# Expert down weights: two neighbouring matrix rows in each partition of a slot, and hidden units transposed in that order

## Chip, cores and metric

The kernel runs on one core of one Trainium2 chip. The metric is the device time of one execution, in microseconds; less is better.

## What is computed

One block of a hybrid backbone on 256 latent tokens and 256 context tokens with a model width of 1024: modulated norm, input projection, retention and latent attention, a gated merge, an output projection with a residual, and then a mixture of experts. The change lies in the experts alone. Each token goes to 4 of 32 experts, and an expert computes, for its tokens xb:

```
gu = xb @ w_gu[e] + b_gu[e]                  # w_gu[e]: 1024 x 2048, gate and up side by side
gate, up = gu[:, :1024], gu[:, 1024:]
gate = minimum(gate, 7);  up = clip(up, -7, 7)
glu = gate * sigmoid(1.702 * gate)
y = ((up + 1) * glu) @ w_down[e] + b_down[e] # w_down[e]: 1024 x 1024
```

The outputs are weighted with the softmax of the four router values, summed per token, added to the residual and normed. All weights are float32, so an expert reads 8 MB for `w_gu` and 4 MB for `w_down`; the 32 experts read 384 MB.

## The kernel before

**Stages.** The program first does modulation, projections, attention, retention, merge, residual and router (up to about 580 us in the profile). Then a loop runs over the 32 experts, one after the other. At the end the last expert's product is done by columns, so that its output can be added and normed in pieces.

**Tokens of an expert.** Each expert has 64 slots for tokens (`CAP`). Matrix products that give 64 rows are paired: one product writes the upper 64 partitions of a PSUM bank and the other the lower 64, with different columns of the weights. So after `gate_up` the tile `up` holds on partitions 0 to 63 the hidden units 0 to 511 of the 64 slots, and on partitions 64 to 127 the units 512 to 1023.

**Weights.** The weights of the experts come in tiles `w` of 128 partitions x 2048 numbers, 1 MB each, twelve per expert. `load_gu` (line 1067) fetches 128 rows of `w_gu`, one row of 8 KB per partition, eight tiles per expert. `load_down` (line 1072) fetches 256 rows of `w_down`, four tiles per expert: rows 256 j to 256 j + 127 go to the first half of the partitions' 8 KB, rows 256 j + 128 to 256 j + 255 to the second half, 4 KB each. The last tile of the last expert is fetched by `load_last` (line 1079) in two DMAs of 512 KB, one for each half. All of these are issued from SP's queue, in the fixed order of the list `todo`: eight gate and up tiles, four down tiles, expert after expert. A tile is fetched when its slot in the ring of buffers (`slots`) is free again; several experts' tiles fit in the ring, so SP runs ahead of the products.

**An expert.** `gate_up` multiplies the gathered tokens with eight tiles (line 1444, eight products a tile), with the previous expert's output added to the tokens on the way (`combine`, line 1426). VectorE and ScalarE then make `up` from the two banks (lines 1448 to 1452). `down` calls `hidden`, which transposes `up` in four blocks of 128 columns on TensorE (the `transpose` of line 147) into one PSUM bank and copies it to the tile `hT` (named `ga`); while these run, TensorE begins the next expert's banks with its biases (line 1307). A block c gives hidden units 128 c on (from the upper slots) and 512 + 128 c on (from the lower ones), one unit per partition, and `hidden` returns the eight 64-column pieces of it in the order of the units. `down` then runs through the four down tiles: half r of tile j is multiplied with piece f = 2 j + r (line 1473, sixteen pairs of products). The last expert uses line 1595 for this in place of line 1473.

**Order.** The order of TensorE's instructions is the order in which the code is written; the other engines' queues are ordered by the framework's scheduler in the expert loop. `order` rows below show both programs' queues.

Of the kernel before, what the change touches and what calls it, by code (L numbers as in the profile page):

```python
# [26 lines left out]
CAP = 64  # L27
# [32 lines left out]
def hybrid_block(ctx: ExitStack, tc: tile.TileContext, A, out, dbg=None):  # L60
# [88 lines left out]
    def rsqrt(p, ss, n, mul, name="rs_y"):  # L149
        """(ss * mul + EPS) ** -0.5"""  # L150
        v = p.tile([128, n], F32, name="rs_v")
        w = p.tile([128, n], F32, name="rs_w")
        y = p.tile([128, n], F32, name=name)
        t = p.tile([128, n], F32, name="rs_t")
        b = p.tile([128, n], I32, name="rs_b")
        nc.vector.tensor_scalar(v, ss, mul, EPS, op0=OP.mult, op1=OP.add)
        nc.vector.tensor_scalar(b, v.bitcast(I32), 1, None, op0=OP.logical_shift_right)
        nc.vector.tensor_scalar(w, v, -0.5, None, op0=OP.mult)
        nc.vector.tensor_tensor(y.bitcast(I32), magic[:, :n], b, op=OP.subtract)
        for _ in range(3):  # L160
            if n > 2:
                nc.vector.tensor_tensor(t, y, y, op=OP.mult)
                nc.vector.tensor_tensor(t, t, w, op=OP.mult)
                nc.vector.scalar_tensor_tensor(y, t, 1.5, y, op0=OP.add, op1=OP.mult)
                continue
            for i in range(n):
                c = slice(i, i + 1)
                nc.vector.scalar_tensor_tensor(t[:, c], y[:, c], w[:, c], y[:, c], op0=OP.mult, op1=OP.mult)
            for i in range(n):
                c = slice(i, i + 1)  # L170
                nc.vector.scalar_tensor_tensor(y[:, c], t[:, c], 1.5, y[:, c], op0=OP.add, op1=OP.mult)
        return y

# [18 lines left out]
    # ada[32 g + r]: (shift, scale) of columns 0.., then 512..; then gate, gate, shift, shift; scale, scale, gate, gate  # L192
# [4 lines left out]
    # The work up to the output projection is a list of steps; those with weights get them loaded and split ahead.  # L197
# [6 lines left out]
    def run_steps():  # L204
        specs = [s for s, _ in steps if s]
        loads = [[]]
        for s in specs:
            loads[-1].append(s)
            if not callable(s):
                loads.append([])  # L210
        loaded, ready = [], []
        at = [0]

        def split_next():
            w, nk, n, raw = loaded[len(ready)]
            if raw:
                ready.append((w,))
            else:
                ready.append([y[:, :nk * n].rearrange("p (k n) -> p k n", k=nk) for y in split(w[:, :nk * n], nk * n)])

        def split_to(n):
            """the next n weights after the current ones, not counting those used as they are"""
            while len(ready) <= at[0]:
                split_next()
            while len(ready) < len(loaded) and sum(len(r) == 2 for r in ready[at[0] + 1:]) < n:
                split_next()

        ahead.append(split_to)
        for spec, fn in steps:
            while len(loaded) < min(at[0] + WR, len(loads) - 1):  # L230
                *others, weight = loads[len(loaded)]
                for other in others:
                    other()
                loaded.append(load(*weight))
            if fn is None:
                continue
            if spec is None:
                fn()
                continue
            split_to(ahead[0])  # L240
            fn(*ready[at[0]])
            at[0] += 1
        steps.clear()

    def load(src, r0, nk, pieces, raw=False):
        """rows r0.. (nk blocks of 128), the columns of all pieces side by side"""
# [72 lines left out]
    def ada_step(q, k):  # L319
        """columns 2048 (q + 1).. of the modulation, rows 128 k.."""  # L320
# [59 lines left out]
    def project(pieces, jobs, kks, mid=None, at=None):  # L380
        """jobs: (bank, part of it, token tile, first column, end column of the loaded ones, starts its bank)"""
# [20 lines left out]
    def matmul2(names, wname, r0, c0, src, k0, first, last):  # L402
        """256 rows from r0 of a weight matrix, 512 columns, against the blocks k0.. of transposed tokens"""
        def f(hi, lo):
            ah, al = src()
            for t in range(2):
                s = slice(128 * t, 128 * t + 128)
                for k in range(2):
                    mm3(B[names[t]], (ah[:, k0 + k, s], al[:, k0 + k, s]), (hi[:, k], lo[:, k]),
                        start=(first and k == 0), stop=(last and k == 1))  # L410
        step(f, (A[wname][0], r0, 2, [(c0, 512)]))
# [13 lines left out]
    def keep_warm(n):  # L425
        """work without a result: TensorE's clock falls while it waits"""
# [53 lines left out]
    M = {}  # L480

    def open_mla():
        dump("mod1", mod1)
        nc.sync.dma_start(tabm, A["tables"][:, 1024:1536])
        # a quarter of the biases of expert e in row 32 q + e
# [113 lines left out]
    def q_up(quad, kks):  # L599
        """queries of four heads: the transposed parts without positions, and the rotated ones"""  # L600
# [42 lines left out]
    def q_rot(pair):  # L643
        """the rotated parts: the high parts in the upper 64 rows, what they lack in the lower"""
# [34 lines left out]
    def scores(pair):  # L679
        """softmax of both heads, for both token tiles"""  # L680
# [83 lines left out]
    def log_decay():  # L764
        """log_sigmoid(r) = min(r, 0) - log1p(exp(-|r|)), log1p(e) = 2 atanh(e / (2 + e))"""
# [41 lines left out]
    def open_ret():  # L807
# [13 lines left out]
        # the normed tokens as rows, in the two parts  # L821
# [14 lines left out]
    def r_rows():  # L836
        """the normed, gated output of a head, transposed and split"""
# [110 lines left out]
    # scores against the normed tokens first, then the value columns of w_in  # L948
# [33 lines left out]
    def gate_ret_out(c):  # L982
        """the heads so far and the other branch, gated; the gate stays for the last head"""
# [72 lines left out]
    slots = []  # L1056

    def add_ring(n, order=None, others=(), **kw):
        """n slots for the experts' weights and others, in the order in which their space gets free"""
# [10 lines left out]
    def load_down(wdn, j):  # L1070
        w = wtile()
        nc.sync.dma_start(w.rearrange("p (r n) -> p r n", r=2),
                          wdn[256 * j:256 * j + 256].rearrange("(r p) n -> p r n", p=128))
        return w

    def load_last(wdn, j):
        w = wtile()
        for r in range(2):
            nc.sync.dma_start(w[:, 1024 * r:1024 * r + 1024], wdn[256 * j + 128 * r:256 * j + 128 * r + 128])
# [11 lines left out]
    def take(f, src, i):  # L1091
        """the next weights of the experts in their order, or others"""
# [79 lines left out]
    def router_weights():  # L1172
        """logits = rstd * (x2 @ (scale * router_w)) + shift @ router_w + router_b"""
# [65 lines left out]
    def split3(parts, src, rest):  # L1239
        """three bfloat16 parts whose sum is src; what is returned does the last two"""  # L1240
# [43 lines left out]
    def one_hot(oh, pos, ne):  # L1284
        """which token is in which slot of ne experts; pos: [128, 2, ne]"""
# [16 lines left out]
    def gu_bias(pick_row):  # L1302
        """banks for the first layer of an expert, begun with its biases; pick_row(q) picks their quarter q"""
# [13 lines left out]
    # top four: all above the fourth value, then the first of those equal to it  # L1317
# [17 lines left out]
    # position of a token among those of its expert, -1 where it isn't sent there  # L1335
# [15 lines left out]
    # gates: softmax over the four  # L1351
# [20 lines left out]
    def slot_scale(oh, ne):  # L1372
        """the norm's factor of the token in each slot, on all partitions"""
# [10 lines left out]
    def gather(oh, rb, xg, k4, ne):  # L1384
        """blocks 4 k4.. of the normed, modulated, transposed tokens in those slots"""
# [23 lines left out]
    def slot_rows(oh, i):  # L1409
        """slots of an expert against tokens, on both halves of the partitions"""  # L1410
# [9 lines left out]
    def combine(ys, ct, g=None, n=CAP):  # L1420
        """add the n rows of the sum of ys to their tokens, weighted with the gates g: [128, 2]"""
# [13 lines left out]
    def gate_up(wgu, halves, xg, i, mid=None):  # L1435
        """one block of CAP tokens of an expert, slot i of xg; mid: other work on the way"""
# [18 lines left out]
    def hidden(up, mid=None):  # L1455
        ps = pt_((128, 4, 128))
        for c in range(4):
            transpose(ps[:, c], up[:, 128 * c:128 * c + 128])
# [18 lines left out]
    def weigh(pys):  # L1477
        """the parts of an expert's output, weighted with the gate of the tokens' update, in two parts"""
# [31 lines left out]
    # biases of the second layer: one more expert whose slots are the experts  # L1510
# [101 lines left out]
    # tokens beyond the first CAP of an expert, CAP at a time  # L1612
# [64 lines left out]
```

## Time and profile before

| what | value |
|---|---|
| time, median of 3 runs | 1525.47 us (1523.48 to 1526.0) |
| span of the profiled execution | 1526.6 us |
| TensorE products busy (ends modelled) | 1427.5 us, 94% |
| VectorE / ScalarE / GpSimd busy | 614.0 / 345.9 / 77.6 us |
| read from memory | 490.02 MB |
| SP's DMA queue, share of the 16 DMA engines' span | 82.1% |
| mean granted clock of TensorE | 0.991 |

The profile has no time of its own beside the span: the span from the first to the last instruction of the profiled execution is 1526.6 us, 1.1 us above the median of the runs, and the time of a run is taken to move as the span does. TensorE's 94% is not a sign that it is the limit: products are pipelined and their ends are modelled, so that a product that is drawn out by a late operand still counts as busy. The shares are means over the whole span, in which the part before the experts and the experts have different limits.

### The profile page before, as it was taken

Reading aid. Unit: us, or ns where it says so; the run is one execution under the profiler, and the core shown is the slowest. Engines: PE = TensorE matmul, PEld = TensorE weight load, DVE = VectorE, ACT = ScalarE, POOL = GpSimd, SP = SyncE. Lnnn points to the kernel's source line nnn. Section 1 sums busy time; section 2 is a strip of 40 time slices with the busy share of each in tenths; the row PEclk is TensorE's granted clock in tenths of the full one; section 3 lists DMA queues with packets and bytes.
Section 4 is the critical chain, followed back from the end, with each engine's and each line's share of the span. In section 5 each row is a group of like instructions: output and inputs, shape, how many; then the busy total and the mean of one; then the engine's idle time right before and its main releaser. Section 6 shows DMA issues by size and latency. Waiting matters only on the chain.

```text
span 1526.6 us, 19528 instructions
## 1 busy us (share of the span) xinstructions
PE 1427.5 (94%) x7977; PEld 761.8 (50%) x7977; DVE 614.0 (40%) x1079; ACT 345.9 (23%) x606; POOL 77.6 (5%) x98
## 2 busy tenths in 40 slices
PE   8999999999999998999999998899898889898985
PEld 4676787888888774333333333333332333233323
DVE  4486645556476573332322332222322232223223
ACT  4354533444344341010110101100110011001001
POOL 3100040101010020000000000000000000000000
PEclk9999999999999999999999999999999999999998
DMA  8635364354548877999999999999999999999994
GB/s 314 200 108 169 135 207 134 111 173 130 170 120 287 314 288 282 415 415 418 416 415 417 416 417 415 416 418 417 415 417 416 417 415 418 417 415 416 417 417 183
DMA packets 117658, 492.42 MB, mean 323 GB/s; under 512 B 9488, under 2 KB 19789, under 8 KB 84793
## 3 DMA queue, kind: packets, MB, share of 16 engines
q1 hardware_dynamic: 116616, 489.23, 82.1%
q0 software_dynamic: 544, 1.21, 0.3%
q8 instruction: 64, 1.05, 0.3%
q10 hardware_dynamic: 400, 0.66, 0.1%
q14 instruction: 34, 0.27, 0.0%
HBM read 490.02 MB, written 1.05 MB: 322 GB/s over the span
## 4 chain that ended last, share of the span: by engine, by line
PE 61%; DMA 29%; DVE 7%; issue 1%; ACT 1%; POOL 0%; DVEq 0%; ACTq 0%; SPq 0%
DMA w<-in_exp_w_gu_dram 26%; PE ps L1444 12%; PE ps L276 9%; PE ps L277 9%; PE ps L278 9%; PE ps L1473 9%; PE ps L1307 4%; PE ps L147 3%; DMA w<-in_exp_w_down_dram 3%; DVE up L1452 1%; DVE up L1450 1%; PE ps L299 1%; PE ps L330 1%; DVE up L1451 1%; PE ps L287 1%
## 5 line engine op out<-in xcount | busy, mean ns | idle before, releaser
L1444 PE MATMUL ps<-w,xg 128*64 128x512 f32 x2048 | 473.6, 599 | 44.8 <-DMA w<-in_exp_w_gu_dram 43.7
L1444 PEld LDWEIGHTS ps<-w,xg 128*64 128x64 f32 x2048 | 134.3, 136 | 361.2 <-issue 215.5
L1473 PE MATMUL ps<-w,ga 128*64 128x512 f32 x992 | 218.7, 593 | 0.0
L268 DVE TENSOR_TENSOR ws<-w,ws 128x1024 fp32r<-128x1024 f32 (+2 forms) x114 | 138.9, 1225 | 74.1 <-ACT ws L267 71.4
L1433 DVE SCALAR_TENSOR_TENSOR x<-ps,gate,x 128x512 f32<-128x512 f32 x124 | 84.5, 744 | 200.2 <-PE ps L1426 200.2
L1473 PEld LDWEIGHTS ps<-w,ga 128*64 128x64 f32 x992 | 71.6, 138 | 142.6 <-issue 140.8
L267 ACT ACTIVATE ws<-w 128x1024 fp32r<-128x1024 f32 (+2 forms) x114 | 116.9, 1027 | 96.9 <-PE ps L278 82.1
L1449 ACT ACTIVATE ps<-ga 128x512 f32<-128x512 f32 x32 | 19.3, 602 | 492.7 <-DVE ga L1448 492.7
L1482 DVE TENSOR_TENSOR ps<-ps,gate 128x512 f32<-128x512 f32 (+1 forms) x33 | 22.6, 684 | 267.3 <-PE ps L1473 258.4
L277 PE MATMUL ps<-ws,hh 128*128 128x512 f32 (+3 forms) x304 | 108.8, 358 | 3.7 <-DVE ws L268 3.7
L276 PE MATMUL ps<-ws,hh 128*128 128x512 f32 (+3 forms) x304 | 109.3, 360 | 0.0
L278 PE MATMUL ps<-ws,hl 128*128 128x512 f32 (+3 forms) x304 | 108.7, 357 | 0.4 <-DVE hl L375 0.4
L1448 DVE TENSOR_SCALAR ga<-ps 128x512 f32<-128x512 f32 x32 | 22.1, 692 | 169.5 <-PE ps L1444 169.5
L272 ACT ACTIVATE up<-ps 128x512 fp32r<-128x512 f32 (+1 forms) x33 | 19.3, 584 | 260.7 <-DVE ps L1482 260.6
L277 PEld LDWEIGHTS ps<-ws,hh 128*128 128x128 f32 x304 | 57.1, 188 | 13.2 <-DVE ws L268 5.0
L276 PEld LDWEIGHTS ps<-ws,hh 128*128 128x128 f32 x304 | 57.1, 188 | 12.8 <-issue 4.4
L1307 PE MATMUL ps<-bgu,ident 128*64 128x512 f32 x256 | 63.2, 615 | 0.0
L278 PEld LDWEIGHTS ps<-ws,hl 128*128 128x128 f32 x304 | 57.1, 188 | 8.2 <-DVE hl L375 0.7
L147 PE MATMUL ps<-ident,up 128*128 128x128 f32 x128 | 20.9, 286 | 22.9 <-DVE up L1452 22.9
L1393 PE MATMUL ps<-oh,acc_m 128*128 128x128 bf16 x512 | 40.5, 223 | 0.0
L278 PE MATMUL ps<-ath,htl 128*128 128x256 f32 x128 | 35.8, 280 | 0.0
L276 PE MATMUL ps<-ath,hth 128*128 128x256 f32 x128 | 35.7, 279 | 0.0
(381 smaller groups left out, 1794.4 us busy)
## 6 DMA issues: line engine op xcount, KB each, us to landing
w<-in_exp_w_gu_dram SPq DMA_DIRECT2D x256, 1024.0 KB, 19.9
w<-in_exp_w_down_dram SPq DMA_DIRECT2D x127, 1024.0 KB, 20.0
w<-in_ada_w_dram SPq DMA_DIRECT2D x48, 512.0 KB, 4.5
w<-in_w_in_dram SPq DMA_DIRECT2D x48, 512.0 KB, 4.3
w<-in_w_in_dram SPq DMA_DIRECT2D x32, 256.0 KB, 5.2
w<-in_w_branch_ret_dram SPq DMA_DIRECT2D x16, 512.0 KB, 4.6
w<-in_w_branch_mla_dram SPq DMA_DIRECT2D x8, 512.0 KB, 5.1
w<-in_w_out_dram SPq DMA_DIRECT2D x8, 512.0 KB, 11.9
```

The lines of the kernel that those rows point to most:

```text
L147: nc.tensor.transpose(dst, src, ident[:n, :n])
L267: nc.scalar.activation(hi[:, :n], src, AF.Copy)
L268: nc.vector.tensor_tensor(lo[:, :n], src, hi[:, :n].bitcast(F32), op=OP.subtract)
L276: nc.tensor.matmul(ps, a[0], b[0], start=start, stop=False, skip_group_check=True)
L277: nc.tensor.matmul(ps, a[0], b[1], start=False, stop=False, skip_group_check=True)
L278: nc.tensor.matmul(ps, a[1], b[0], start=False, stop=stop, skip_group_check=True)
L1307: nc.tensor.matmul(ps[64 * h:64 * h + 64], pick_row(c // 512).to_broadcast([128, CAP]), bgu, start=True, stop=False, skip_group_check=True)
L1393: nc.tensor.matmul(ps[:, i, :w], part[:, t, ks], rhs, start=(t + p + i == 0), stop=(t + p == 3), skip_group_check=True)
L1433: nc.vector.scalar_tensor_tensor(a, pss[h], g[:, t:t + 1], a, op0=OP.mult, op1=OP.add)
L1444: nc.tensor.matmul(ps[64 * h:64 * h + 64], xg[k // 4][:, k % 4, sl], w[:, c:c + 512], start=False, stop=(k == KD - 1), skip_group_check=True)
L1473: nc.tensor.matmul(py[64 * h:64 * h + 64], hT[f], w[:, 1024 * r + 512 * h:1024 * r + 512 * h + 512], start=(f == 0), stop=(f == KD - 1))
L1482: nc.vector.tensor_tensor(py, py, gate2[:, cs], op=OP.mult)
```

## The change

`load_down` takes 256 consecutive rows of `w_down` as pairs: partition p gets rows 256 j + 2 p and 256 j + 2 p + 1, which lie beside each other in memory, as one run of 8 KB. `load_last` does the same in its two halves: its first DMA takes the even rows of the 256, the second the odd ones, each row still 4 KB. Since half r of a tile now holds the rows 256 j + 2 p + r, the hidden units have to stand on the partitions in that order: `hidden` transposes, for block c, every second column of `up`, starting at column 256 (c // 2) + c % 2, in place of 128 consecutive columns. The pieces, the products and their number stay. The changed file has no comments and doc strings, which shifts no line before `hidden` and two lines behind it.

```diff
     def load_down(wdn, j):
         w = wtile()
-        nc.sync.dma_start(w.rearrange("p (r n) -> p r n", r=2),
-                          wdn[256 * j:256 * j + 256].rearrange("(r p) n -> p r n", p=128))
+        nc.sync.dma_start(w, wdn[256 * j:256 * j + 256].rearrange("(p r) n -> p (r n)", r=2))
         return w

     def load_last(wdn, j):
         w = wtile()
+        rows = wdn[256 * j:256 * j + 256].rearrange("(p r) n -> p r n", r=2)
         for r in range(2):
-            nc.sync.dma_start(w[:, 1024 * r:1024 * r + 1024], wdn[256 * j + 128 * r:256 * j + 128 * r + 128])
+            nc.sync.dma_start(w[:, 1024 * r:1024 * r + 1024], rows[:, r])
         return w
...
     def hidden(up, mid=None):
         ps = pt_((128, 4, 128))
+
+        pairs = up.rearrange("s (j p r) -> s j r p", j=2, r=2)
         for c in range(4):
-            transpose(ps[:, c], up[:, 128 * c:128 * c + 128])
+            transpose(ps[:, c], pairs[:, c // 2, c % 2])
         if mid:
             mid()
```

No instruction is added, removed or moved on any engine. On SP's queue, where the experts' first down tile stands between the last tiles of the output projection (`w_out`, line 258), the DMA of line 1072 has another shape:

```order
 L258 DMA w_4841<-in_w_out_dram 128x2x512
 L1067 DMA w<-in_exp_w_gu_dram 128x2048 x2
-L1072 DMA w<-in_exp_w_down_dram 128x2x1024
+L1072 DMA w<-in_exp_w_down_dram 128x2048
 L258 DMA w_4963<-in_w_out_dram 128x2x512
 L258 DMA w_4980<-in_w_out_dram 128x2x512
```

The tile is written as one run of 2048 numbers per partition, which is the shape of the gate and up tiles of line 1067; its place in the queue is the old one.

On TensorE's queue, at the place where an expert's `hidden` and `down` meet the next expert's `gate_up`, the rows are these (`ident` is the unit matrix, `bgu` the biases, `ga` the tile hT):

```order
 L147 MATMUL ps<-ident,up 128x128 x4
 L1307 MATMUL ps<-bgu,ident 64x512 x4
-L1473 MATMUL ps<-w,ga 64x512 x16
+L1475 MATMUL ps<-w,ga 64x512 x16
 L1444 MATMUL ps<-w,xg 64x512 x16
 L1426 MATMUL ps<-up,ct 128x512 x2
```

Only the line's number differs. The four transposes of line 147 stand where they did, with the same shapes; that they read every second number of `up` does not show in the rows.

## Rows read from the trace of the kernel before

**Rows 1.** The page: the span, and DMA load in 40 slices.
```profile
span 1526.6 us, 19528 instructions
...
DMA  8635364354548877999999999999999999999994
GB/s 314 200 108 169 135 207 134 111 173 130 170 120 287 314 288 282 415 415 418 416 415 417 416 417 415 416 418 417 415 417 416 417 415 418 417 415 416 417 417 183
```

**Rows 2.** The chain, 1000 to 1070 us: start, length, what.
```profile
1021.76 19.88 DMA w<-in_exp_w_gu_dram
...
1051.87 19.91 DMA w<-in_exp_w_gu_dram
```

**Rows 3.** DMA packets by size; DMA issues: count, KB each, us to landing.
```profile
DMA packets 117658, 492.42 MB, mean 323 GB/s; under 512 B 9488, under 2 KB 19789, under 8 KB 84793
...
w<-in_exp_w_gu_dram SPq DMA_DIRECT2D x256, 1024.0 KB, 19.9
w<-in_exp_w_down_dram SPq DMA_DIRECT2D x127, 1024.0 KB, 20.0
```

**Rows 4.** Waits of SP's queue: us in total, times, longest.
```profile
SPq L1072 <- DMA w<-in_exp_w_gu_dram: 218.6, 106, 3.4
SPq L1067 <- DMA w<-in_exp_w_down_dram: 215.7, 106, 3.6
```

**Rows 5.** SP's issues, one tile each: start, length of the issue, line.
```profile
589.40 0.34 SPq L1067 DMA_DIRECT2D w<-in_exp_w_gu_dram  x1
...
1004.42 4.11 SPq L1067 DMA_DIRECT2D w<-in_exp_w_gu_dram  x1
...
1011.58 0.56 SPq L1067 DMA_DIRECT2D w<-in_exp_w_gu_dram  x1
...
1021.76 0.33 SPq L1067 DMA_DIRECT2D w<-in_exp_w_gu_dram  x1
...
1024.25 0.38 SPq L1072 DMA_DIRECT2D w<-in_exp_w_down_dram  x1
...
1031.72 1.83 SPq L1072 DMA_DIRECT2D w<-in_exp_w_down_dram  x1
```

**Rows 6.** Two stretches: us, then busy us (count) by engine, clock, DMA share, GB/s.
```profile
656.75:673.75 17.00, 17.00 (x84) 5.87 (x82) 3.43 (x6) 0.71 (x2) 0.00 (x0) 1.00 1.01 416
...
779.00:794.50 15.50, 14.53 (x94) 5.99 (x92) 6.93 (x12) 2.26 (x5) 0.00 (x0) 1.00 1.02 421
```

**Rows 7.** Two other stretches, the same columns.
```profile
767.25:774.50 7.25, 7.25 (x36) 2.43 (x34) 1.39 (x2) 0.60 (x1) 0.00 (x0) 1.00 1.03 408
...
1041.50:1045.75 4.25, 3.83 (x42) 2.40 (x42) 2.63 (x4) 1.07 (x3) 0.00 (x0) 1.00 1.03 411
```

**Rows 8.** Two stretches at the start of the experts, the same columns.
```profile
580.00:590.00 10.00, 10.00 (x67) 4.77 (x66) 2.84 (x8) 1.99 (x5) 0.00 (x0) 0.94 0.45 138
590.00:600.00 10.00, 9.78 (x54) 3.59 (x50) 3.87 (x7) 1.40 (x4) 0.00 (x0) 1.00 1.03 419
```

**Rows 9.** The chain, 600 to 700 us, at the transposes.
```profile
628.04 0.66 PE ps L147 x4
...
654.76 0.66 PE ps L147 x4
```

**Rows 10.** Groups by line, 900 to 1490 us.
```profile
L1444 PE MATMUL ps<-w,xg 128*64 128x512 f32 x1250 | 297.1, 602 | 43.6 <-DMA w<-in_exp_w_gu_dram 42.6
...
L147 PE MATMUL ps<-ident,up 128*128 128x128 f32 x76 | 12.4, 286 | 14.7 <-DVE up L1452 14.7
...
L147 PEld LDWEIGHTS ps<-ident,up 128*128 128x128 f32 x76 | 7.9, 140 | 18.0 <-DVE up L1452 15.5 <-issue 2.4
```

**Rows 11.** The chain in the last expert.
```profile
1476.86 19.86 DMA w<-in_exp_w_gu_dram
...
1501.79 0.44 PE ps L147 x4
...
1503.13 6.65 PE ps L1595 x60
```

## Prediction

> **What bounds the kernel now.** I read the page's slices first [rows 1]. Up to slice 16 (610 us; a slice is 38.2 us) the DMA engines are half idle; from there to the end they are 90% busy or more and move 415 to 418 GB/s in every full slice, whatever the other engines do. A rate that stays this flat over 23 slices is a limit of its own, so I looked at the experts as a stream of DMAs. Two stretches at its start show where it becomes full: 138 GB/s from 580 to 590 us, 419 GB/s in the ten microseconds after [rows 8]. The 25th issue of an expert's tile is at 589.40 [rows 5], so the tiles of the first two experts (24) came mostly ahead of the full stream, and all from the third expert on are in it.
>
> The chain says the same in the middle of the experts: a last gate and up tile is issued at 1021.76 and lands 19.88 us later, the next expert's is issued at 1051.87 and takes 19.91 [rows 2]. One expert thus takes 1071.78 - 1041.64 = 30.14 us, or 2.51 us for each of twelve tiles of 1 MB, and the 19.9 us in which a tile is on its way are eight such steps: eight tiles are queued. What releases SP is in its waits: line 1072 waits for gate and up tiles and line 1067 for down tiles, 106 times each [rows 4], that is, an issue waits for the landing of the tile eight issues before it.
>
> Is TensorE near that limit? Early in the loop, while it still lives on tiles fetched ahead, it goes from one expert's transposes to the next's in 654.76 - 628.04 = 26.72 us [rows 9], which is its own pace. Later it waits for the tiles: 42.6 us in 590 us, some 2.2 us per expert by a view that counts drawn-out products as busy [rows 10]. So the experts are bound by the DMA stream, with TensorE some 3 us per expert below it.
>
> **Part one: the down tiles as runs of 8 KB.** The tiles of both matrices have the same bytes, but not the same packets. Of 117658 packets 32865 are of 8 KB or more; the gate and up tiles account for 256 x 128 = 32768 of them, so they travel as one packet per partition and the down tiles as two of 4 KB [rows 3]. Does that cost time? The steps of SP's queue give the landings one by one. The issue at 1011.58 was released by the last gate and up tile, the one at 1021.76 by the fourth down tile after it, the one at 1031.72 by the fourth gate and up tile of the next expert [rows 5]. Four down tiles took 10.18 us, 2.545 each; four gate and up tiles took 9.96 us, 2.490 each. That is 0.055 us for each down tile. The period gives a second value: twelve tiles at 2.490 would take 29.88 us, against 30.14 that is 0.26 per expert or 0.065 per down tile. I take 0.0575, nearer to the direct one, because the period also holds the steps in which both kinds are under way.
>
> A third view bounds it. In ten stretches in which the packet records are of 8 KB alone the rate is 416 to 421 GB/s; in nine with 4 KB alone it is 408 to 411; the lowest and the highest of each stand in [rows 6, 7]. A megabyte takes 2.521 to 2.491 us in the first and 2.570 to 2.551 in the second, so the difference lies between 0.030 and 0.079 us.
>
> After the change the DMA of line 1072 has the destination of line 1067, and its source is 1 MB without a gap, as that of line 1067; I give it the step of 2.490. Which tiles count? Those of experts 3 to 31: 29 x 4 = 116. Those of the first two came ahead of the full stream, and those of the last expert are not waited for: its last gate and up tile lands at 1476.86 + 19.86 = 1496.72, TensorE begins the down products at 1503.13 and runs them in 6.65 us with no wait in the chain [rows 11]. So the gain is 116 x 0.0575 = 6.7 us, and 116 x 0.030 = 3.5 to 116 x 0.079 = 9.2 at its bounds.
>
> The Trainium skill has a figure for the same thing: DMA: Bandwidth & Descriptors, Why small descriptors are slow, gives each packet a fixed overhead of about 3 cycles inside the DMA engine. At the 850 MHz fabric clock of the same page of the skill I estimate 3.5 ns a packet; a DMA engine is spared eight packets per tile, 0.028 us, and the sum by it would be 3.3 us. The rows above have about twice as much, and the measurement decides.
>
> **Part two: issues.** An issue of SP mostly takes 0.33 us for a gate and up tile and 0.38 for a down tile, but 1.83 where the fourth down tile goes out and 4.11 just behind one [rows 5]. If these long ones come from the many packets of the queued down tiles, they get short. They cost nothing now and give nothing: the tile issued last in such a stretch still has six or seven ahead of it in the queue, some 15 us of cover, and the rate does not dip.
>
> **Part three: the transposes read every second column.** There are four per expert, 0.66 us together on the chain [rows 9], with a weight load of 140 ns each [rows 10]. No row shows an operand with such a step. Below, the cost is zero; above, I take the load twice as long, 4 x 0.14 = 0.56 us per expert, the price if every number took the place of two. In the experts of the stream this is hidden behind the wait for the tiles, some 2 us per expert; without that cover it would be 29 x 0.56 = 16 us. On the path it stands once, in the last expert [rows 11]: 0 to 0.56 us. I take zero, since the transpose itself counts as 286 ns and the load lies mostly under the product ahead of it.
>
> **Part four: the last tile.** `load_last` keeps two DMAs with 4 KB rows, now every second row of the source. The products of that tile come last of the four, some 5 us behind 1503.13; this has no share in the sum.
>
> **The sum.** 6.7 us off the median of 1525.47 gives 1518.8 us; the profiled execution's span would go from 1526.6 to 1519.9. About 0.2%, or 3 us, is what a measurement of this kernel can tell from no change.
>
> **Rivals.**
> *The same rate for both (0.09).* The 4 KB packets may not be why the down tiles are slow: they move while VectorE turns one expert into the next, and the two could disturb each other in the on-chip memory; or the chip cuts runs of the new kind so that the change does nothing. Then the time stays at 1525.5, give or take 3 us. For it: the difference is only 2%, and two things differ between the stretches. Against it: VectorE is busy for 6.93 of 15.50 us in a fast stretch at 421 GB/s and for 1.39 of 7.25 us in a slow one at 408 [rows 6, 7], and the packet counts show that runs of 8 KB stay whole. The Trainium skill has a rule for this rival, in DMA: Bandwidth & Descriptors, Specifications: line rate from 512 B on, by which both sizes run alike and nothing changes; the trace does not agree, with 408 to 411 against 416 to 421 GB/s.
>
> *TensorE becomes the bound, slower (0.03).* If a step of two made each transpose five times as long, an expert would cost 4 x 0.66 = 2.64 us more on TensorE. At its own pace TensorE would get from the second expert's transposes (628.04) to the last expert's in 30 x 26.72 = 802 us, that is to 1429.6; in fact they are at 1501.79 [rows 9, 11]. The room is 72 us, 2.4 us per expert; 2.64 would use it up and cost 30 x 0.24 = 7 us, the gain being lost too: 1532.7. It decides from 2.4 us per expert or 0.6 us a transpose, four times the bound above. The Trainium skill speaks against it too: SBUF — State Buffer, in Door 1, wants two hits in each 16-byte line, and a step of 8 bytes has two. No run here shows that yet.
>
> *More than the bounds (0.02).* Should the stream lose other stops with the extra packets, the gain could pass 9.2 us: 1515.
>
> **Numbers.** The forecast, a gain of 3 to 9.2 us, has the rest, 0.86. Its ends are the bounds of the rate, less the 0.56 us of the last transposes at the low end: 1525.5 - 9.2 = 1516.3, and 1525.5 - 3.5 + 0.6 = 1522.6. That alone holds more than 8 in 10, so the range is 1516.3 to 1522.6. Faster by over 0.2%: the forecast and the last rival, 0.88; within 0.2%: 0.09; slower: 0.03.
>
> **What the changed profile would show.** Packets under 8 KB fall by 127 x 256 = 32512, and those of 8 KB or more rise by 16256. The GB/s of the full slices go from 416 to about 420. The landings step by 2.49 us throughout and an expert takes 29.9 us. The long issues of SP shorten. TensorE's transposes stay at 0.66 us; its wait for gate and up tiles falls by about 0.2 us per expert. The prediction is wrong if the down tiles keep a step of 2.54 with 8 KB packets (then it was not the packets), or if the step falls and the period does not, which would mean that something other than the stream sets the experts' pace; a transpose group of 3 us would point to TensorE.

## The result

| kernel | time, us | ratio to before, 95% interval |
|---|---|---|
| before | 1524.63 (1523.48 to 1526.0, 5 runs) | |
| changed | 1517.21 (1515.29 to 1519.66, 5 runs) | 0.9944 [0.9922, 0.9966] |

The changed kernel is 7.4 us faster by the medians; 0.56% of 1524.63, by the ratio, is 8.5 us, with an interval of 5.2 to 11.9. The profiled execution's span is 8.7 us shorter. 1518.8 us was predicted, within 1516.3 to 1522.6. A run's time is 1.8 us more than its span (1519.66 us for the span of 1517.9), so both profiled executions are longer than the medians of their kernels: some 1528.4 us for the kernel before, 1519.66 for the changed one.

The page of the changed kernel: the span, the rate in 40 slices and the packets by size.

```profile
span 1517.9 us, 19528 instructions
...
GB/s 316 201 108 165 138 210 126 112 180 125 171 121 278 312 302 265 419 419 421 420 420 420 420 420 420 421 420 420 420 420 419 421 420 420 420 420 421 420 420 184
DMA packets 101401, 492.42 MB, mean 324 GB/s; under 512 B 9487, under 2 KB 19788, under 8 KB 52280
```

From slice 17 on the full slices move 419 to 421 GB/s, where they moved 415 to 418 [rows 1]. There are 16257 packets fewer in all and 32513 fewer under 8 KB [rows 3]: two packets of 4 KB became one of 8 KB, 127 x 128 = 16256 times; one packet is left over.

The issues on SP's queue, start and length, one tile each; the first was released by the landing of an expert's last gate and up tile, the second by its fourth down tile, the third by the fourth gate and up tile of the next expert, the last by that expert's eighth.

```profile
1037.31 0.33 SPq L1067 DMA_DIRECT2D w<-in_exp_w_gu_dram  x1
...
1047.26 0.33 SPq L1067 DMA_DIRECT2D w<-in_exp_w_gu_dram  x1
...
1057.23 0.33 SPq L1072 DMA_DIRECT2D w<-in_exp_w_down_dram  x1
...
1067.17 0.33 SPq L1067 DMA_DIRECT2D w<-in_exp_w_gu_dram  x1
```

Four down tiles now land in 1047.26 - 1037.31 = 9.95 us, where they took 10.18 [rows 5]; the next four gate and up tiles in 9.97 (9.96 before). A whole expert takes 1067.17 - 1037.31 = 29.86 us against 30.14 [rows 2]. All twelve tiles have the same step of 2.49 us.

The same issues over the whole program (minimum, median and maximum in ns ahead of the comma), of the changed kernel:

```profile
L1067 SPq DMA_DIRECT2D w<-in_exp_w_gu_dram x256: 327/328/987, 458.1 to 1468.6; - x128
```

and of the kernel before:

```profile
L1067 SPq DMA_DIRECT2D w<-in_exp_w_gu_dram x256: 327/328/4218, 458.4 to 1476.9; - x128
```

The issues of up to 4.2 us are gone [rows 5]; the longest takes 1.0.

TensorE in the experts, groups of 900 to 1490 us of the changed kernel: busy time, mean of one, idle time and what ended it.

```profile
L1444 PE MATMUL ps<-w,xg 128*64 128x512 f32 x1280 | 302.9, 601 | 35.7 <-DMA w<-in_exp_w_gu_dram 34.4
...
L147 PE MATMUL ps<-ident,up 128*128 128x128 f32 x76 | 14.2, 309 | 14.7 <-DVE up L1452 14.7
...
L147 PEld LDWEIGHTS ps<-ident,up 128*128 128x128 f32 x76 | 10.6, 209 | 18.0 <-DVE up L1452 15.5 <-issue 2.4
```

The weight load of a transpose (the row of LDWEIGHTS) takes 209 ns where it took 140, the transpose counts as 309 against 286 [rows 10]. The wait for gate and up tiles is 34.4 us, 8.2 less. The chain at the transposes of the second and third expert and in the last one:

```profile
627.50 0.74 PE ps L147 x4
...
654.31 0.74 PE ps L147 x4
```

```profile
1468.60 19.84 DMA w<-in_exp_w_gu_dram
...
1493.52 0.53 PE ps L147 x4
...
1494.94 6.65 PE ps L1597 x60
```

The four transposes take 0.74 us in place of 0.66, and TensorE's own pace is 654.31 - 627.50 = 26.81 us an expert, 0.09 more than before [rows 9]. In the last expert the chain is the old one [rows 11]: last gate and up tile, transposes (0.53, was 0.44), down products without a wait. That tile lands at 1488.44, 8.3 us sooner. Not all of this is the stream's: SP's 25th issue of an expert's tile, at 589.40 before [rows 5], is now at 588.76, and the first one of all already came 0.35 us sooner in this execution (458.07, before 458.43).

```profile
588.76 0.33 SPq L1067 DMA_DIRECT2D w<-in_exp_w_gu_dram  x1
```

### The profile page after: what moved, and what is told of

It is laid out like the page before. It is cut to its first block, busy times and chain, and to the rows that moved or that the text cites. A ratio compares the mean times of both kernels' runs of the same rounds, so it can differ in the third digit from the quotient of the medians.

```text
span 1517.9 us, 19528 instructions
## 1 busy us (share of the span) xinstructions
PE 1428.5 (94%) x7977; PEld 766.9 (51%) x7977; DVE 613.8 (40%) x1079; ACT 345.9 (23%) x606; POOL 77.6 (5%) x98
## 4 chain that ended last, share of the span: by engine, by line
PE 50%; DMA 42%; DVE 5%; issue 1%; ACT 1%; POOL 0%; ACTq 0%; DVEq 0%; SPq 0%
DMA w<-in_exp_w_gu_dram 29%; DMA w<-in_exp_w_down_dram 13%; PE ps L276 9%; PE ps L277 9%; PE ps L278 9%; PE ps L1444 9%; PE ps L1475 4%; PE ps L147 3%; PE ps L1307 1%; PE ps L299 1%; PE ps L330 1%; PE ps L287 1%; PE ps L428 1%; PE ps L1426 1%; DVE up L1452 1%
## 5 line engine op out<-in xcount | busy, mean ns | idle before, releaser
L1444 PE MATMUL ps<-w,xg 128*64 128x512 f32 x2048 | 472.4, 598 | 35.7 <-DMA w<-in_exp_w_gu_dram 34.4
L1464 ACT ACTIVATE ga<-ps 128x512 f32<-128x512 f32 x32 | 19.1, 597 | 74.5 <-PE ps L147 74.5
```

Source lines behind the costliest of these rows:

```text
L1444: nc.tensor.matmul(ps[64 * h:64 * h + 64], xg[k // 4][:, k % 4, sl], w[:, c:c + 512], start=False, stop=(k == KD - 1), skip_group_check=True)
```

## The experiments

The theory is that a packet costs a DMA engine a fixed time whatever it carries, that the experts' stream is bound by these engines, and that the change therefore saves the time of eight packets per engine in each down tile of the stream. The rivals: the distance of a partition's two rows in memory was the cost, not the size of the packets; the transposes' step takes part in it; TensorE is on the path after all. For all of them the rate of the stream is read from one stretch, 640 to 1480 us: length, busy time and count of TensorE's products, its weight loads, VectorE, ScalarE and GpSimd, then clock, DMA share, GB/s. Each ratio is to runs of the kernel before that were made beside the kernel's own (medians 1525.01 to 1525.25 us). These are the kernel before and the changed one:

```profile
640.00:1480.00 840.00, 774.60 (x4218) 281.52 (x4214) 234.97 (x385) 83.95 (x185) 0.00 (x0) 1.00 1.02 416
...
640.00:1480.00 840.00, 783.39 (x4252) 289.14 (x4250) 236.26 (x387) 84.56 (x186) 0.00 (x0) 1.00 1.01 420
```

**Each half of the change alone.** First the DMAs without the step of the transposes:

```diff
-        pairs = up.rearrange("s (j p r) -> s j r p", j=2, r=2)
         for c in range(4):
-            transpose(ps[:, c], pairs[:, c // 2, c % 2])
+            transpose(ps[:, c], up[:, 128 * c:128 * c + 128])
```

> The changed DMAs with the transposes of before (128 neighbouring columns); the hidden units then meet the wrong rows of the down weights, and only the time is read. Theory (the stream of 8 KB packets carries the whole gain): 1517 us, a step of 2.49 us for every tile, the four transposes back at 0.66 us, SP's issues all at 0.33 us. Rival (the transposes' step costs something that the shorter stream hid): some us below the changed kernel, 1515 or less.

1516.69 us, ratio 0.9947 [0.9934, 0.9960]. The stretch:

```profile
640.00:1480.00 840.00, 780.35 (x4252) 285.69 (x4252) 237.88 (x390) 84.47 (x186) 0.00 (x0) 1.00 1.01 420
```

Then the transposes of the change with the DMAs of before (the opposite edit, on the kernel before):

> The changed transposes (every second column) with the DMAs of before; hidden units and weight rows do not match, and only the time is read. Theory: 1524.6 us, within 1 us of before; the weight loads of line 147 go from 140 to 209 ns and the four transposes from 0.66 to 0.74 us, hidden behind the wait for tiles except once at the end. Rival (the step is part of the gain, or a cost): over 3 us away from before.

1526.52 us, ratio 1.0008 [0.9993, 1.0024].

```profile
640.00:1480.00 840.00, 777.34 (x4220) 286.29 (x4218) 234.94 (x385) 83.97 (x185) 0.00 (x0) 1.00 1.02 416
```

The DMAs alone bring the whole gain and the rate of 420 GB/s; the transposes alone change nothing that can be told from before (the median is 1.4 us above its own before, and the interval holds 1), at 416. The step of the transposes has no part in the gain, and its own cost does not show in the time.

**Packets or places.** Two kernels take the two apart. Both read a pair of tiles from 512 rows, so that a partition's rows lie close together. In the first the tile holds rows 4 p + 2 r + i, two pieces of 4 KB:

```diff
+        rows = wdn[512 * (j // 2):512 * (j // 2) + 512].rearrange("(p r i) n -> p i r n", r=2, i=2)
-        nc.sync.dma_start(w, wdn[256 * j:256 * j + 256].rearrange("(p r) n -> p (r n)", r=2))
+        nc.sync.dma_start(w.rearrange("p (r n) -> p r n", r=2), rows[:, j % 2])
```

> Down tiles of two 4 KB pieces per partition that lie close together in memory: rows 4 p + 2 r + i of 512, transposes with a step of four. Packets as small as before, but the source as local as in the changed kernel. Theory (each packet costs a fixed time): as before, 1524.6 us, down tiles with a step of 2.55 us, long issues on SP as before. Rival (the two pieces 512 KB apart were the cost): as the changed kernel, 1517 us, step 2.49.

1527.72 us, ratio 1.0020 [1.0011, 1.0028].

```profile
640.00:1480.00 840.00, 775.32 (x4216) 285.54 (x4214) 235.37 (x386) 83.88 (x185) 0.00 (x0) 1.00 1.02 416
```

In the second it holds rows 4 p + 2 i + r, one run of 8 KB out of every 16 KB:

```diff
+        rows = wdn[512 * (j // 2):512 * (j // 2) + 512].rearrange("(p i r) n -> p i (r n)", i=2, r=2)
-        nc.sync.dma_start(w, wdn[256 * j:256 * j + 256].rearrange("(p r) n -> p (r n)", r=2))
+        nc.sync.dma_start(w, rows[:, j % 2])
```

> Down tiles of one 8 KB run per partition, but every second 8 KB of the source only: rows 4 p + 2 i + r of 512, transposes with a step of four. Theory (packets alone): as the changed kernel, 1517 us, step 2.49. Rival (a source without gaps is what is faster): slower than the changed kernel by 3 us or more, towards 1524.

1517.24 us, ratio 0.9951 [0.9938, 0.9963].

```profile
640.00:1480.00 840.00, 783.17 (x4256) 289.64 (x4254) 238.25 (x390) 84.53 (x186) 0.00 (x0) 1.00 1.01 420
```

Small packets from near places run at 416, large ones with gaps at 420. The size of the packets decides, and the place, at the distances tried, does not; nor does VectorE, which is busy for 235.37 us of the one stretch and 238.25 of the other. The first of the two is even some 3 us slower than before; its stream has the rate of before and its profiled span is no longer (1525.3, before 1526.6), so the profile does not hold those 3 us, and where they lie was not found.

**Still smaller packets.** Four pieces of 2 KB per partition:

```diff
+        half = wdn[512 * (j // 2):512 * (j // 2) + 512].rearrange("(p q) (c n) -> p c q n", q=4, c=2)
-        nc.sync.dma_start(w, wdn[256 * j:256 * j + 256].rearrange("(p r) n -> p (r n)", r=2))
+        nc.sync.dma_start(w.rearrange("p (q n) -> p q n", q=4), half[:, j % 2])
```

> Down tiles of four 2 KB pieces per partition, all of them from a local source; the numbers are not those that the products need, and only the time is read. Theory: a packet costs a DMA engine a fixed time of some 8 ns (0.066 us per down tile for eight packets more), so 24 packets more than the changed kernel's cost 0.20 us a tile, a step of 2.69 us, and 116 x 0.20 = 23 us: 1540 us. Rival (4 KB is a special size, say from how pieces are cut or queued, and no fixed cost stands behind it): 1525 us or less.

1542.47 us, ratio 1.0112 [1.0095, 1.0129]: 25 us above the changed kernel, against the 23 expected.

```profile
640.00:1480.00 840.00, 768.54 (x4158) 279.17 (x4154) 232.22 (x381) 82.50 (x182) 0.00 (x0) 1.00 1.02 408
```

4 KB is no special size. At 408 GB/s a megabyte takes 2.570 us in the mean, at 420 it takes 2.497; twelve tiles make 0.88 us per expert, and with four down tiles and 24 packets more in each, a packet costs 9 ns. From 416 to 420 it is 12 x (2.521 - 2.497) / 32, also 9 ns; these rates are whole GB/s, and by the megabytes that each stretch moved it is 9.2 ns (342.75 MB here, 352.85 in the changed kernel) and 8.4 (349.73 in the kernel before).

**How much room TensorE has.** Each transpose of the changed kernel is done three and five times into the same place (the edit for three; for five the loop runs to 20):

```diff
-        for c in range(4):
-            transpose(ps[:, c], pairs[:, c // 2, c % 2])
+        for c in range(12):
+            transpose(ps[:, c % 4], pairs[:, c % 4 // 2, c % 2])
```

> The changed kernel with each of the four transposes of an expert done three times into the same place: 1.48 us more of TensorE's time per expert. Theory: TensorE's own pace goes from 26.8 to 28.3 us per expert, still below the 28.87 us that the stream leaves it on average (from the second expert's transposes at 627.5 to the last one's at 1493.5), so the time stays within 1 us of the changed kernel, 1517 us. Rival (TensorE is on the path in the experts): 1517 + 31 x 1.48 = 1563 us, or a good part of that.

1519.02 us, ratio 0.9959 [0.9945, 0.9973]. That is 1.8 us above the changed kernel, where at most 1 was expected; about 1 us of it is the last expert's own transposes, which take 1.49 us in place of 0.53.

> The same with each transpose five times: 2.96 us more per expert. Theory: TensorE's own pace is now 29.8 us, the bound goes over to TensorE, the last expert's transposes come at 627.5 + 30 x 29.8 = 1521 in place of 1493.5: 27 us more, 1544 us. Rival (there is more room than that): 1517 us.

1522.28 us, ratio 0.9982 [0.9972, 0.9993]: 5 us above the changed kernel, where 27 were expected. The chain at the second and third expert, of the first kernel and of the second, and the second's group of line 1444 and its last transposes:

```profile
627.53 1.71 PE ps L147 x12
...
655.32 1.71 PE ps L147 x12
```

```profile
627.18 2.67 PE ps L147 x20
...
655.93 2.67 PE ps L147 x20
```

```profile
L1444 PE MATMUL ps<-w,xg 128*64 128x512 f32 x1334 | 294.7, 594 | 0.5 <-DMA w<-in_exp_w_gu_dram 0.5
```

```profile
1493.88 2.45 PE ps L147 x20
```

The price in my expectation was wrong: I had taken a further transpose at 0.74 / 4 = 0.185 us, and sixteen more made 2.67 - 0.74 = 1.93, 0.12 each. With that the mechanism fits: TensorE's pace goes to 655.93 - 627.18 = 28.75 us an expert, just under the 28.87 that the stream leaves it, its wait for tiles falls from 34.4 to 0.5 us, and the last transposes begin where they did (1493.88, 1493.52 before the edit). 1.9 us of the 5 are the last expert's own transposes on the chain (2.45 against 0.53). The two profiles differ by 2.3 us in all (1520.2 and 1517.9), so the rest of the 5 lies in the runs and not in these profiles, and was not found. So TensorE has room for some 2 us per expert in the changed kernel, and is not what bounds it.

**Larger packets.** Two kernels have slots of 16 KB, eight in all (16 MB of tiles in place of 21). One fills a slot by one DMA of 2 MB, the other by two of 1 MB with 8 KB runs. The loads of the first:

```diff
+    def load_gu2(wgu, k):
+        w = wtile()
+        nc.sync.dma_start(w, wgu[256 * k:256 * k + 256].rearrange("(p r) n -> p (r n)", r=2))
+        return w
+
+    def load_down2(wdn, j):
+        w = wtile()
+        nc.sync.dma_start(w, wdn[512 * j:512 * j + 512].rearrange("(p r) n -> p (r n)", r=4))
+        return w
```

> Slots of 16 KB per partition, eight in all in place of twenty-one of 8 KB; a DMA brings 2 MB, two rows of the gate and up weights or four of the down weights in one run of 16 KB per partition. The gate and up rows are not the ones that the tokens' blocks need, and only the time is read; the smaller ring costs lead at the start. Theory (a fixed cost per packet, 8 ns): four packets fewer per megabyte and engine, 2.457 us a megabyte in the stream against 2.49 of the next kernel. Rival (no cost left from 8 KB on): 2.49 in both.

> The same slots of 16 KB, each filled by two DMAs of 1 MB with 8 KB runs, in the order of rows that the products need for both matrices: the comparison for the kernel with 16 KB runs. Theory: 2.49 us a megabyte in the stream.

1517.98 us, ratio 0.9949 [0.9932, 0.9966], with 16 KB runs; 1533.42 us, ratio 1.0046 [1.0034, 1.0058], with two of 8 KB. The second is 16 us slower than the changed kernel with the same 8 KB runs, and the first gets 15.4 of it back. The stretch of the one and of the other:

```profile
640.00:1480.00 840.00, 772.28 (x4250) 292.94 (x4250) 237.43 (x389) 84.58 (x186) 0.00 (x0) 1.00 1.01 427
```

```profile
640.00:1480.00 840.00, 774.14 (x4186) 282.54 (x4184) 234.97 (x385) 83.95 (x185) 0.00 (x0) 1.00 1.01 420
```

At 427 GB/s a megabyte takes 2.456 us, 0.041 less than at 420; with four packets fewer that is 10 ns each, and the step expected was 2.457. The DMAs of the first kernel are also twice as large, 2 MB in place of 1, and that was not taken apart from the packets. What the trace says is where the time was saved. These are the DMA queue's packets, megabytes and share of the 16 engines' time in the stretch, for the first kernel and the second:

```profile
q1 hardware_dynamic: 24585, 357.92, 100.4%
...
q1 hardware_dynamic: 48336, 351.98, 101.0%
```

In engine time a million bytes cost 16 x 840 x 1.004 / 357.92 = 37.7 us in the first and 38.6 in the second: the saving lies inside the packets' own times, not in pauses between DMAs.

The 16 us are not lost in the stretch, where the second kernel runs at the 420 of the changed one. Its last gate and up tile lands at 1479.44 + 19.89 = 1499.33, 10.9 us later than the changed kernel's:

```profile
1479.44 19.89 DMA w<-in_exp_w_gu_dram
```

Beside the ring's size, a slot there comes free only when both of its tiles are done, and the last tile is not fetched in halves; which of these costs what was not tested.

**A version that beats both.** This points to 16 KB runs in every expert tile with as much ring as fits, and the model's columns ordered so that partition p of a block holds column 256 m + 2 p + r. The ring has ten slots of 16 KB, not the nine of the expectation: 3, 1, 4 and 1, and one more in the tile `both`, which is made large enough for it and handed over as `halves[:1]`. The core of the edit beside the two loads above:

```diff
-RINGS = 4, 3, 9, 1
+RINGS = 3, 1, 4, 1
...
-        both = halves[q].tile([128, 2, KD // 2, T], F32R, name="w")
+        both = halves[q].tile([128, 2 if q else 4, KD // 2, T], F32R, name="w")
...
-    add_ring(RINGS[2], (1, 8, 2, 3, 4, 9, 0, 5, 6, 7, 10), halves)
+    add_ring(RINGS[2], (1, 4, 0, 2, 3), halves[:1])
...
-                transpose(ps[:, j], x[:, t, cs][:, 128 * j:128 * j + 128])
+                transpose(ps[:, j], x[:, t, cs].rearrange("s (j p r) -> s j r p", j=2, r=2)[:, j // 2, j % 2])
...
-        pairs = up.rearrange("s (j p r) -> s j r p", j=2, r=2)
+        fours = up.rearrange("s (p r) -> s r p", r=4)
```

> A whole kernel with 16 KB runs in every expert tile: nine slots of 16 KB in place of twenty-one of 8 KB, two rows of the gate and up weights or four of the down weights per partition, and the model's columns ordered to match (router weights, second norm's gain, modulation, the split tokens and their transposes). Theory: the stream at 427 GB/s gives 15 us against 8 KB runs; the ring holds 18 MB in place of 21, some 3 x 2.5 = 7.5 us less lead; 1517.2 - 15 + 7.5 = 1510 us. Rival (the smaller ring or the steps in the token order eat it): 1517 us or more.

1509.91 us (1509.38 to 1510.42), ratio 0.9902 [0.9886, 0.9919]. Its page:

```profile
span 1508.7 us, 19146 instructions
...
GB/s 318 203 109 158 138 221 115 123 182 112 182 126 221 341 226 312 425 427 427 427 426 427 426 428 427 428 426 428 426 428 425 428 427 428 427 426 427 428 427 150
DMA packets 73638, 492.39 MB, mean 326 GB/s; under 512 B 6427, under 2 KB 16732, under 8 KB 48968
```

It is 15 us faster than before and 7 us faster than the changed kernel, with a stream of 425 to 428 GB/s. That it came out at the expected 1510 is partly luck: with ten slots (20 MB) the same working takes off 2.5 us of lead in place of 7.5 and gives 1517.2 - 15 + 2.5 = 1504.7, and where the other 5 us went was not found.

## Why the prediction was right, and where it was not

The bound, the cost and the way that the time moved were right. The step of the prediction that failed is the size of one term of its sum: the gain per down tile, taken as 0.0575 us, was 0.067.

**The bound.** Right. The stream moves at a flat rate before and after, the step per tile fell and the period with it, and TensorE waited less. (Its wait for gate and up tiles fell by 8.2 us in some 20 experts, 0.4 each, where I had written 0.2.) TensorE's own pace of 26.81 us is 3 us below the stream's period of 29.86, and 2 us below the 28.87 that an expert has on average, the tiles fetched ahead included; the kernel with five transposes used these 2 us up.

**The gain per down tile.** The mechanism is right, and the term was too small. The direct step fell from 2.545 to 9.95 / 4 = 2.488, by the 0.0575 us that I took. But over the whole stretch the rate gives more. The packets of 640 to 1480 us, before and after:

```profile
DMA packets 62314, 349.73 MB, mean 416 GB/s; under 512 B 5322, under 2 KB 5322, under 8 KB 33994
...
DMA packets 48416, 352.85 MB, mean 420 GB/s; under 512 B 5378, under 2 KB 5379, under 8 KB 5379
```

A tile of 1 MB (1.0486 million bytes) goes from 2.5185 to 2.4963 us in the mean; twelve tiles make 0.267 per expert, or 0.067 per down tile. That is close to the 0.065 of the period, which I had set aside in part "because the period also holds the steps in which both kinds are under way". By the rows of one expert those steps gain a little as well. In the kernel before, SP's issues that were released by an expert's last gate and up tile, by its fourth down tile, and by the fourth and the eighth gate and up tile of the next expert are these:

```profile
1041.70 1.21 SPq L1067 DMA_DIRECT2D w<-in_exp_w_gu_dram  x1
...
1051.87 0.33 SPq L1067 DMA_DIRECT2D w<-in_exp_w_gu_dram  x1
...
1061.85 2.76 SPq L1072 DMA_DIRECT2D w<-in_exp_w_down_dram  x1
...
1071.84 0.57 SPq L1067 DMA_DIRECT2D w<-in_exp_w_gu_dram  x1
```

The steps are 10.17, 9.98 and 9.99 us, against 9.95, 9.97 and 9.94 after: the gate and up tiles have 0.06 of the 0.28. A likely reason, which no run shows by itself, is that the DMA engines do not change from one kind to the other together: the stretches of down packets alone are 7.25 and 4.25 us long, though four down tiles take 10.2 [rows 7], so that an engine still at its 8 KB packets and one already at the small ones may work on the same landing.

With 0.067 the sum is 116 x 0.067 = 7.8 us in place of 6.7. With the 0.64 us by which the 25th issue came sooner that makes 8.4, and the last gate and up tile comes 8.3 us sooner. The span's 8.7 us hold 0.5 more, which arise behind the down products (1503.13 to the end at 1526.6, and 1494.94 to 1517.9). The 0.64 and the 0.5 have no term in the sum, and whether they belong to the change or to these two executions is open. The bounds of 3.5 to 9.2 held the gain.

**Which tiles count.** Right as far as the rows show: with 116 tiles the stream's gain comes out as the landings have it, the first experts' tiles come ahead of the full stream, and in the last expert the down products run without a wait in both chains.

**Packets, not places.** The argument from VectorE's busy time and from the whole 8 KB runs was right, and the two kernels with near small and gapped large pieces show it. The rival of one rate for both is out: the stretch runs at 408 and 416 GB/s with the down tiles in packets of 2 and 4 KB, at 420 with all tiles in 8 KB, and at 427 in 16 KB.

**The fixed cost.** The runs show 8 to 10 ns a packet, at 2 and 4 against 8 KB, and at 16 KB as far as the size of the DMAs has no part in it. The Trainium skill, DMA: Bandwidth & Descriptors, Why small descriptors are slow, has a cost of this kind; my estimate from its 3 cycles was 3.5 ns a packet and 3.3 us in all, less than half of what was measured. The Trainium skill's line rate from 512 B on, in DMA: Bandwidth & Descriptors, Specifications, does not hold for this stream: its rate still rises from 2 to 16 KB.

**Issues.** Right: with 8 KB packets the long issues are gone, and with the small near ones they were as in the kernel before (up to 4.1 us):

```profile
L1067 SPq DMA_DIRECT2D w<-in_exp_w_gu_dram x256: 327/328/4105, 458.4 to 1476.0; - x128
```

Up to 8 KB, long issues and small packets go together in every run. Two things speak against the issues as the cost. The DMA share of the stretch is 1.02 in the kernels with long issues and 1.01 in the changed one, so the engines were no less busy where the issues were long; and of the two kernels with 16 KB slots neither has an issue above 0.8 us, and their rates still differ, 420 and 427 GB/s.

**The transposes.** I took zero, for the load would lie under the product ahead, and wrote that they would stay at 0.66 us; they take 0.74, and 0.09 us is on the chain in the last expert. This is a second, small miss, towards a slower kernel. The bound of 0.56 held. The slower rival, TensorE as the bound, did not happen; its deciding point of 2.4 us was close to the room of about 2 us that the repeated transposes found.

## What to carry to other kernels

Where a stretch is bound by its DMAs at a flat rate, look at the size of the packets, not only of the transfers: DMAs of 1 MB with runs of 2, 4 and 8 KB moved at different rates here, and those of 2 MB with 16 KB runs faster still. A layout that lets a partition take neighbouring rows costs little if the order of the other operand can be changed on the way (here 0.09 us on the chain). Count what larger runs cost in buffers: the step from 8 to 16 KB was worth 15 us, and the slots that it needed cost 16 us where the ring shrank from 21 to 16 MB. Price a per-tile gain by the period of the loop, or the rate over many turns of it, since a step between two landings of one kind misses what the transition gains.

## What the hardware showed that I had not expected

A packet cost the DMA engines about the same, 8 to 10 ns, whether it carried 2, 4 or 8 KB, and 8 KB runs still lost 1.6% against 16 KB in larger DMAs (420 and 427 GB/s).

Reading every second float32 column made a weight load 209 ns in place of 140. A step of four columns cost the load no more, as the kernel with near 4 KB pieces shows (minimum, median, maximum in ns):

```profile
L147 PEld LDWEIGHTS ps<-ident,up x128: 195/209/221, 596.6 to 1501.0; 128*128 128x128 f32 x128
```

The Trainium skill, SBUF — State Buffer, in Door 1, speaks of full rate with two hits in each 16-byte line; by that a step of two would have been free. The rows have it at 209 ns, and a step of four, with one hit a line, no slower.
